# A hybrid GLA/HGRN2 layer on one core: the gate path ahead of the output projection, and the projection of two tiles by seven block products

## The chip, the cores and the metric

The kernel runs on one core of one Trainium2 chip. The metric is the device time of one execution in microseconds (us), lower is better. Each kernel was run several times; the profile is of one execution, taken by the hardware profiler. Five engines work beside each other, each on its own instructions in a fixed order: TensorE (PE; its weight loads are PEld), VectorE (DVE), ScalarE (ACT), GpSimd (POOL) and SyncE (SP), which only issues DMAs here.

## The reference

One inference step of a streaming encoder layer over 4096 prompt frames and 64 sample frames, width 1024, all in fp32. What matters for this change is its end:

```python
p = jnp.einsum('btd,de->bte', h, w_in)
q_a, k_a, v_a, z_a, a_lr, q_h, f_h, i_h, z_h = jnp.split(p, ...)
...                       # two gated recurrences give o_a and o_h, 512 wide each
o_a = rms_norm(o_a, g_on_gla).reshape(B, T, GLA_V) * jax.nn.silu(z_a)
o_h = rms_norm(o_h, g_on_hgrn).reshape(B, T, HGRN_W) * jax.nn.silu(z_h)
o = jnp.einsum('bte,ed->btd', jnp.concatenate([o_a, o_h], axis=-1), w_out)
y = x + gate[:, None] * rms_norm(o, g_post)
```

## The kernel before

Tokens are worked in 16 groups of 256, each two tiles of 128 tokens; the 64 sample frames ride as a third tile beside one group, so there are 33 tiles. Matrix products of fp32 data are made of three matmuls in a faster format, fp32r: each operand is split into a high part, rounded on ScalarE (`split`, L92), and a low part, the remainder, by a subtraction on VectorE or GpSimd (L93); high x high, high x low and low x high are summed in PSUM. With a gain the split is L89 on ScalarE and L90 on VectorE. For the half-full sample tile high and low part lie side by side in one operand, so that two matmuls do the work of three (`pair_step`), and `fold` adds the halves.

The program has three phases. The first runs the GLA heads over all groups, the second the HGRN2 heads; both write their outputs, normalised and (GLA) gated, to DRAM (`oa_d`, `oh_d`), and the normalised input is kept split-ready in DRAM as `h_d`. While a group's projections run, generators of other work are woven between them (`weave`: so many steps of a side, between so many steps of the main work). Phase 3 is the end: for each tile the projection z_h with its SiLU (`z_tile`: 24 matmuls of 512 columns from L620, sigmoid L1244, product L1245), the product with o_h (L1295), eight transposes (L1303), a split with the norm's gain (L89, L90), and the output projection, two halves of 512 columns with 24 matmuls each (L1338), square for the norm (L1343), scaling with gate (L1347), reciprocal root (`rstd`), product and residual (L1350) and store (L1352 or L1354).

The head of phase 3: four gate tiles are made while the last attention side of phase 2 and `load_wout` are woven in. `load_wout` loads w_out in 16 half rows of 128x512 (L1256) through a staging buffer `wst` and splits each, high part on ScalarE, low part on GpSimd, into eight units `wv` and eight `wu`. Then `phase3` alternates: one gate tile, then one tile's projection.

The framework's scheduler sets the order of each engine's instructions when the program is built; on the chip every engine runs its order, and waits where a semaphore is not there yet. All loads go through SyncE's queue in its order. Buffers come from pools of a fixed number of tiles: `hh` (split of a group's input, four used per group, five buffers), `hf` (its loads), PSUM banks `pj` (3), `at` (2), `tp`, `ms` and `o` (1 each), and the weight staging pool with two buffers of 128x1056, each of which serves two half rows.

In the profile's rows tiles are named without their number, so `wu` stands for all units of that name; L93 is the low part of a split, whatever is split. The lines are of this kernel; the new code's lines are those of the kernel after, where `split` is L93 and L94.

Of the kernel before, what the change touches and what calls it, by code (L numbers as in the profile page):

```python
# [28 lines left out]
class Kernel:  # L29
# [102 lines left out]
    def wunit(self, tag):  # L132
        return self.wpool.tile([P, 1056 if tag == "wv" else 1024], F32R, name=tag, bufs=8 if tag == "wv" else 16)


    def setup(self):
# [4 lines left out]
        self.wstage = self.pool(ctx, "wstage", 2)  # L141
        self.halves = []
        self.xp = self.pool(ctx, "x")
        self.hp = self.pool(ctx, "h")
        self.ep = self.pool(ctx, "e")
# [71 lines left out]
    def first_group(self, ap, ada, w, rows):  # L217
# [66 lines left out]
        def w_split(i, w):  # L284
            W[("qk", "z")[i]].append(self.split_w(w[i], ("wu", "wv")[i]))
# [62 lines left out]
        vs = self.weights(W["v"], C_VA, 512, "wu", self.etile, 3)  # L348
# [887 lines left out]
    def z_tile(self, h, r, o):  # L1236
        nc = self.nc
        pz = self.ps(self.z_bank)
        for _ in self.proj_tok(pz, self.W3["z"], 0, 512, h, o, r):
            yield  # L1240
# [8 lines left out]
    def load_wout(self, out):  # L1249

        sts = []
        for i in range(2 * KT + 2):
            if i < 2 * KT:
                kt, n = divmod(i, 2)
                st = self.wst()[:, :512]
                self.nc.sync.dma_start(st, self.t["w_out"][0, kt * P : (kt + 1) * P, 512 * n : 512 * n + 512])  # L1256
                sts.append(st)
            if i >= 2:
# [3 lines left out]
    def og_load(self, tile, og):  # L1262

        g, j, (kind, _, r, _) = tile
        g = g if kind == "p" else -1
        self.nc.sync.dma_start(og[:r, :512], self.oa_d[g][j])
        self.nc.sync.dma_start(og[:r, 512:], self.oh_d[g][j])

    def phase3(self, tiles, zgen, og):
        nc, t = self.nc, self.t  # L1270
        with ExitStack() as s:
            one = self.pool(s, "p3one")
            ap = self.pool(s, "p3a")
            gg = one.tile([P, 2, D], F32, name="gg")
            for i in range(2):
                nc.sync.dma_start(gg[:, i, :], self.gate_d[i : i + 1, :].to_broadcast([P, D]))
            Wo = self.W3["o"]
            og0 = og

            def load(i):  # L1280
                g, j, (kind, r0, r, o) = tiles[i]
                if i > 0:
                    og = ap.tile([P, D], F32, name="og", bufs=2)
                    self.og_load(tiles[i], og)
                else:
                    og = og0
                xt = self.xp.tile([P, D], F32, name="xt", bufs=2)
                src = t["x_prompt"] if kind == "p" else t["x_sample"]
                nc.sync.dma_start(xt[:r], src[0, r0 : r0 + r, :])
                return og, xt  # L1290

            def turn(i, og):
                r = tiles[i][2][2]
                e = self.zq.pop(0)
                nc.vector.tensor_tensor(og[:r, 512:], og[:r, 512:], e, ALU.mult)  # L1295
                hi = ap.tile([P, D], F32R, name="ogh", bufs=2).rearrange("p (k c) -> p k c", k=KT)
                lo = None
                if r == P:
                    lo = ap.tile([P, D], F32R, name="ogl", bufs=2).rearrange("p (k c) -> p k c", k=KT)
                for q, tag in enumerate(("tp", "ms")):  # L1300
                    pt = self.ps(tag).rearrange("p (k c) -> p k c", k=4)
                    for k in range(4):
                        nc.tensor.transpose(  # L1303
                            pt[:, k, :r], og[:r, (4 * q + k) * P : (4 * q + k + 1) * P], self.ident[:r, :r]
                        )
                    ks = slice(4 * q, 4 * q + 4)
                    self.split(hi[:, ks, :r], lo[:, ks, :r] if r == P else hi[:, ks, r : 2 * r], pt[:, :, :r], gain=self.col[:, 50 + q : 51 + q])
                return hi, lo

            n = len(tiles)  # L1310
            og, xt = load(0)
            next(zgen, None)
            hl = turn(0, og)
            for i in range(n):
                g, j, (kind, r0, r, o) = tiles[i]
                dst = t["y_prompt"] if kind == "p" else t["y_sample"]
                x_now, (hi, lo) = xt, hl
                if i + 1 < n:
                    next(zgen, None)
                    og, xt = load(i + 1)  # L1320
                    hl = turn(i + 1, og)
# [222 lines left out]
```

## Time and profile before

| what | value |
|---|---|
| time, median of 3 runs | 2156.81 us (2154.11 to 2157.73) |
| profiled execution | 2156.92 us |
| its span, first to last instruction | 2155.1 us |
| mean granted TensorE clock | 0.994 |
| bytes moved by DMA | 173.22 MB, mean 80 GB/s |
| last TensorE instruction of the output projection | starts at 2147.43 us of the span |
| last store issued | 2151.99 us |

The page's busy shares say how much of the span an engine works; the stretches (windows) say the same for parts of it, with the number of instructions in brackets. In a timeline row the columns are start, duration, engine, line, operation, output <- inputs, shape and count, and in square brackets the idle time ahead and what ended it. Matmul ends are modelled and overlap, so their pace is read from starts. A group's row ends with busy time in us and the mean of one in ns. A wait's row has total, count and longest in us.

### The profile page before, as it was taken

To read this page: it belongs to the slowest core of one execution; us is meant where nothing else is said; L and a number is where in the kernel's file an instruction comes from. 1 tells how busy PE (TensorE), PEld (TensorE's weight loads), DVE (VectorE), ACT (ScalarE), POOL (GpSimd) and SP (SyncE) were. 2 spreads that over 40 slices of the span, in tenths; PEclk is the share of its full clock that TensorE was granted. 3 is DMA by queue.
4 is the path that set the end of the run, shared out by engine and by line. 5 is a ranking of instruction groups with operands and counts; after the bars stand their busy time and mean duration, and the time that the engine had idled before them with its cause. 6 is when DMAs were issued, how large, how long until landed. Compare 5 with 4: busy or idle time off the path is not lost.

```text
span 2155.1 us, 44875 instructions
## 1 busy us (share of the span) xinstructions
PE 2109.0 (98%) x16574; PEld 1854.7 (86%) x16574; DVE 1502.3 (70%) x4851; ACT 993.3 (46%) x2960; POOL 234.2 (11%) x640
## 2 busy tenths in 40 slices
PE   8999999999999999999999999999999999999998
PEld 6888998889988888989999899999878888888887
DVE  6777777777777778787788887777895454545444
ACT  5666655666556654444444444444542222222212
POOL 3200010000100111110001110000240000000000
PEclk9999999999999999999999999999999999999999
DMA  9322222222222321012211101011253333334322
GB/s 262 112 58 74 63 58 50 66 66 62 57 50 62 111 93 47 31 31 70 65 51 45 36 31 50 31 36 43 91 161 130 120 123 108 127 115 131 110 100 88
DMA packets 218632, 173.22 MB, mean 80 GB/s; under 512 B 136236, under 2 KB 158224, under 8 KB 218412
## 3 DMA queue, kind: packets, MB, share of 16 engines
q1 hardware_dynamic: 218268, 170.08, 26.5%
q8 instruction: 131, 2.15, 0.4%
q14 instruction: 89, 0.73, 0.1%
q10 hardware_dynamic: 144, 0.26, 0.0%
HBM read 118.35 MB, written 51.93 MB: 79 GB/s over the span
## 4 chain that ended last, share of the span: by engine, by line
PE 82%; DVE 10%; ACT 4%; DMA 1%; issue 1%; SPq 1%; POOL 0%; DVEq 0%; ACTq 0%; POOLq 0%
PE ps_pj L620 22%; PE ps_pj L608 20%; PE ps_pj L1338 16%; PE ps_at L620 7%; PE ps_ms L840 2%; PE ps_o L824 2%; PE ps_o L819 2%; DVE wst L910 2%; PE ps_at L687 2%; PE ps_at L959 2%; PE ps_at L767 1%; PE ps_tp L794 1%; PE ps_tp L1303 1%; DVE dd L693 1%; PE ps_ms L1303 1%
## 5 line engine op out<-in xcount | busy, mean ns | idle before, releaser
L620 PE MATMUL ps_pj<-wu,hh 128*128 128x512 f32 x1632 | 405.2, 398 | 3.1 <-DVE hh L93 2.3
L608 PE MATMUL ps_pj<-hh,wu 128*128 128x256 f32 (+1 forms) x2976 | 392.1, 287 | 0.0
L608 PEld LDWEIGHTS ps_pj<-hh,wu 128*128 128x128 f32 x2976 | 372.8, 191 | 4.9 <-issue 0.3
L620 PEld LDWEIGHTS ps_pj<-wu,hh 128*128 128x128 f32 x1632 | 297.9, 188 | 65.8 <-issue 3.3
L608 PE MATMUL ps_pj<-hh,wv 128*128 128x256 f32 (+1 forms) x1536 | 214.7, 291 | 0.0
L608 PEld LDWEIGHTS ps_pj<-hh,wv 128*128 128x128 f32 x1536 | 193.2, 190 | 12.1 <-issue 9.3
L620 PE MATMUL ps_pj<-wv,hh 128*128 128x264 f32 x1464 | 199.3, 290 | 1.6 <-DVE wv L93 1.6
L620 PEld LDWEIGHTS ps_pj<-wv,hh 128*128 128x128 f32 x1464 | 184.1, 188 | 6.8 <-issue 2.4
L1343 ACT ACTIVATE sq<-ps_pj 128x512 bf16<-128x512 f32 (+1 forms) x66 | 39.4, 597 | 295.8 <-PE ps_pj L1338 294.3
L1338 PE MATMUL ps_pj<-wv,ogh 128*128 128x512 f32 x512 | 162.9, 399 | 0.0
L1338 PE MATMUL ps_pj<-wu,ogh 128*128 128x512 f32 x512 | 158.0, 390 | 0.0
L620 PE MATMUL ps_at<-wu,hh 128*128 128x512 f32 x672 | 157.7, 390 | 0.0
L1204 ACT ACTIVATE g<-ps_pj 128x256 f32<-128x256 f32 (+1 forms) x128 | 49.5, 387 | 229.5 <-PE ps_pj L608 228.8
L620 PEld LDWEIGHTS ps_at<-wu,hh 128*128 128x128 f32 x672 | 126.3, 188 | 26.1
L92 ACT CAST hh<-hf 128x512 fp32r<-128x512 f32 (+1 forms) x188 | 117.1, 626 | 68.5 <-PE ps_pj L620 38.7
L93 DVE TENSOR_TENSOR hh<-hf,hh 128x512 fp32r<-128x512 f32 (+1 forms) x188 | 130.7, 703 | 15.7 <-ACT hh L92 14.9
L941 POOL COPY T<-T 128x16 f32<-128x16 f32 (+1 forms) x32 | 9.9, 309 | 996.9 <-DVE Qg L880 893.2
L1338 PEld LDWEIGHTS ps_pj<-wu,ogh 128*128 128x128 f32 x512 | 96.1, 188 | 20.7
L1338 PEld LDWEIGHTS ps_pj<-wv,ogh 128*128 128x128 f32 x512 | 94.3, 189 | 19.3
L910 DVE TENSOR_TENSOR wst<-wst,T 128x160 f32<-128x160 f32 (+3 forms) x480 | 108.4, 267 | 1.1
L1338 PE MATMUL ps_pj<-wv,ogl 128*128 128x512 f32 x256 | 100.8, 394 | 0.0
L1338 PE MATMUL ps_pj<-wu,ogl 128*128 128x512 f32 x256 | 99.7, 390 | 0.0
(303 smaller groups left out, 3745.8 us busy)
## 6 DMA issues: line engine op xcount, KB each, us to landing
hf<-h_d SPq DMA_DIRECT2D x128, 256.0 KB
xt<-in_x_prompt_dram SPq DMA_DIRECT2D x36, 512.0 KB
h_d<-hf SPq DMA_DIRECT2D x64, 256.0 KB
out_y_prompt_dram<-y SPq DMA_DIRECT2D x31, 512.0 KB
xt<-in_x_prompt_dram SPq DMA_DIRECT2D x448, 32.0 KB
wst<-in_w_in_dram SPq DMA_DIRECT2D x36, 256.0 KB
ada_st<-in_w_ada_dram SPq DMA_DIRECT2D x32, 256.0 KB
oa_d<-e SPq DMA_DIRECT2D x32, 256.0 KB
```

Source lines behind the costliest of these rows:

```text
L92: self.nc.scalar.copy(hi, src)
L93: (eng or self.nc.vector).tensor_tensor(lo, src, hi.bitcast(F32), ALU.subtract)
L608: self.nc.tensor.matmul(ps[:, :T], a, b, start=i == 0, stop=i == n - 1)
L620: self.nc.tensor.matmul(ps[:r, : c1 - c0], a, b, start=kt == 0 and i == 0, stop=kt == KT - 1 and i == 2)
L687: nc.tensor.transpose(pt[:, i * P : (i + 1) * P], D[:, c + i, :], self.ident)
L819: nc.tensor.matmul(po[h], A[:, c * 4 + h, :], v, start=h < n, stop=St is None and h == 4 - n)
L824: nc.tensor.matmul(o, Q[rows[s], c * G + g, :], St[rows[s], g, :], start=NS == 2 and not apart and h == 1, stop=h == 4 - NS or h == 3 and ...
L840: nc.tensor.matmul(pd[s * w : (s + 1) * w, g, :], kc[:CL, g, s * w : (s + 1) * w], vs[c][:CL, h * P : (h + 1) * P], start=not apart, stop= ...
L910: nc.vector.tensor_tensor(parts(dst), parts(src), t.unsqueeze(3).to_broadcast(shape), ALU.mult)
L959: nc.tensor.matmul(pas[s][rows, g0 + g], K[rr, 2 * pr + g, rows], Yt[rr, o : o + P], start=True, stop=True)
L1204: nc.scalar.activation(sg, pf[:, :T], AF.Sigmoid)
L1338: nc.tensor.matmul(po[:r], a[:, kt, :r], b, start=m == 0, stop=m == 3 * KT - 1)
```

## The change

Phase 3 falls into two parts.

*Gate part.* All 33 gate tiles run one behind the other. Each loads its tile of o_h from DRAM, multiplies it by SiLU(z_h), and stores it back to the same place. Eight tiles are woven with the last attention side (spread over more steps than before); then 22 more are woven with `load_wout`. It now loads, for each of four block rows, two rows of 128x1024 (L1284), scales them by the norm's gain on ScalarE (L1285), takes four differences of their 512-wide halves on GpSimd (L1290) and splits seven operands (L93 on ScalarE, L94 on GpSimd): B11, B21, B22, T1, T2, T3, T4. That makes 28 units, 8 in `wv`, 8 in `wb` and 12 in `wc`. Of the differences each overwrites one of the staging buffers' halves.

*Projection.* Two tiles (256 tokens) are one 2x2 block matrix A (rows: the tiles; columns: GLA half and HGRN2 half), and w_out with its gain is a 2x2 block matrix B. Instead of eight block products, seven are made, each of 12 matmuls of 512 columns (L1336), of A's blocks and of sums of blocks: S1 = A21 + A22, S2 = S1 - A11, S3 = A11 - A21, S4 = A12 - S2. Sixteen transposes (L1327) bring the blocks to PSUM; VectorE makes the sums (L1357, L1363), and the results are put together from the products by additions from PSUM (L1408). The low parts of S1, S3 and S4 and two of the four scalings are on GpSimd, the rest on VectorE. Squares (L1396), scalings (L1399), the reciprocal root, now from ScalarE's table, product and residual (L1417) and stores of 512 columns (L1418) follow as before. The sample tile is projected inside the last pair with the prepared operands, in 40 matmuls instead of 32.

The buffers move as well: `wu` with 16 units becomes `wa` with 8 and `wb` with 8, some pools are allocated from the other side of the memory, and the pools of x and h are closed early to make room.

The diff, cut to its core:

```diff
-    def z_tile(self, h, r, o):
+    def z_tile(self, h, tile):
...
+        oh = self.etile()[:r]
+        nc.sync.dma_start(oh, o_d)
+        pz = self.ps("pj")
+        yield from self.proj_tok(pz, self.W3["z"], 0, 512, h, o, r)
...
         nc.vector.tensor_tensor(e, pz[:r], e, ALU.mult)
-        self.zq.append(e)
+        nc.vector.tensor_tensor(oh, oh, e, ALU.mult)
+        nc.sync.dma_start(o_d, oh)
...
-                st = self.wst()[:, :512]
-                self.nc.sync.dma_start(st, self.t["w_out"][0, kt * P : (kt + 1) * P, 512 * n : 512 * n + 512])
...
-                out.append(self.split_w(sts[i - 2], "wv" if i - 2 < 8 else "wu", self.nc.gpsimd))
...
+                st = self.stage_pair()[:, :D]
+                nc.sync.dma_start(st, self.t["w_out"][0, (4 * q + kt) * P : (4 * q + kt + 1) * P, :])
+                nc.scalar.activation(st, st, AF.Copy, scale=self.col[:, 50 + q : 51 + q])
...
+        for kt in range(4):
+            b11, b12, b21, b22 = load(kt)
...
+                self.split(us[n][:, 0], us[n][:, 1], src, nc.gpsimd)
...
+            put("B11", b11)
+            sub(b11, b12, b11)
+            sub(b12, b22, b12)
+            yield
+            put("B22", b22)
+            put("B21", b21)
+            sub(b22, b22, b11)
+            sub(b21, b21, b22)
+            yield
+            for n, src in (("T1", b11), ("T3", b12), ("T2", b22), ("T4", b21)):
+                put(n, src)
...
+        def product(bank, u, name):
+            for kt in range(4):
+                for i, (a, b) in enumerate(((0, 0), (0, 1), (1, 0))):
+                    nc.tensor.matmul(bank, u[:, a, kt, :], W[name][kt][:, b], start=kt + i == 0, stop=kt + i == 5)
...
+                product(b, cur["A11"], "B11")
...
+                product(b, cur["A12"], "B21")
+                y11 = add(self.etile(), b, p1)
+                square(ss[0], 0, y11)
+                scale(y11, y11, 0, eng=nc.gpsimd)
...
+                    parts(S3, w3, nc.gpsimd)
+                    parts(S1, w1, nc.gpsimd)
+                    parts(S2, w2)
...
+                product(b, cur["S2"], "T2")
+                u2 = add(tmp(), b, p1)
...
+                product(b, cur["S3"], "T3")
+                u3 = add(tmp(), b, u2)
...
+                    parts(S4, w4, nc.gpsimd)
...
+                product(b, cur["S1"], "T1")
+                y22 = add(self.etile(), b, u3)
...
+                scale(y22, y22, 1, eng=nc.gpsimd)
+                u4 = add(tmp(), b, u2)
...
+                product(b, cur["S4"], "B22")
+                y12 = add(self.etile(), b, u4)
...
+                product(b, cur["A22"], "T4")
+                y21 = add(self.etile(), b, u3)
...
-            self.weave(until(4), [(side, 15, 0, 12), (self.load_wout(W3["o"]), 18, 0, 12)])
...
+            self.weave(until(8), [(side, 15, 0, 22)])
...
+            self.weave(until(len(tiles) - 3), [(self.load_wout(room), 16, 0, 56)])
+            ogs = [self.og_half(0, j, q, self.ep if j else None) for j in range(2) for q in range(2)]
+            now(until(len(tiles) - 1))
+            self.project(ogs, lambda: now(zg))
```

More of the change, by code (lines that the diff above doesn't have):

```diff
@@ L1262, in og_load @@
[L1262 to L1270, printed above, removed]
-        with ExitStack() as s:
[L1272 to L1299, printed above, removed]
-                for q, tag in enumerate(("tp", "ms")):
[L1301 to L1305, printed above, removed]
-                    ks = slice(4 * q, 4 * q + 4)
[L1307 to L1321, printed above, removed]
-                cnd = 0 if kind == "p" else 1
-                ss = self.small.tile([P, 2], F32, name="y_ss")[:r]
-                y = ap.tile([P, D], F32, name="y", bufs=2)
-                if i == n - 1:
-                    self.tc.keep_in_program_order(nc.scalar.preload_act_table_set("natural_log_exp_and_others"))
@@ new lines, in load_wout, with unit, load, sub @@
+    def load_wout(self, room):
+        nc = self.nc
+        W = self.W3
+        names = ("B11", "B21", "B22", "T1", "T2", "T3", "T4")
+        for n in names:
+            W[n] = []
+        rooms = [("wv", i) for i in range(8)] + [("wb", i) for i in range(8)]
+        def unit():
+            u = self.wunit(rooms.pop(0)[0]) if rooms else room.tile([P, 1024], F32R, name="wc", bufs=12)
+            return u[:, :1024].rearrange("p (two c) -> p two c", two=2)
+        def load(kt):
+            sts = []
+            for q in range(2):
+                st = self.stage_pair()[:, :D]
+                nc.sync.dma_start(st, self.t["w_out"][0, (4 * q + kt) * P : (4 * q + kt + 1) * P, :])
+                nc.scalar.activation(st, st, AF.Copy, scale=self.col[:, 50 + q : 51 + q])
+                sts += [st[:, :512], st[:, 512:]]
+            return sts
+        def sub(dst, a, b):
+            nc.gpsimd.tensor_tensor(dst, a, b, ALU.subtract)
+        for kt in range(4):
+            b11, b12, b21, b22 = load(kt)
+            yield
+            us = {n: unit() for n in names}
+            def put(n, src):
+                self.split(us[n][:, 0], us[n][:, 1], src, nc.gpsimd)
[10 more added lines that the diff above has]
+                put(n, src)
+            for n in names:
+                W[n].append(us[n])
+            yield
@@ L1328, in phase3 @@
                 for q in range(2):
                     po = self.ps("pj")
-                    cs = slice(512 * q, 512 * q + 512)
-                    m = 0
-                    for kt in range(KT):
-                        wh, wl = Wo[2 * kt + q][:, 0], Wo[2 * kt + q][:, 1]
-                        if r < P:
-                            self.pair_step(po, hi[:, kt, : 2 * r], r, wh, wl, kt)
-                            continue
-                        for a, b in ((hi, wh), (hi, wl), (lo, wh)):
-                            nc.tensor.matmul(po[:r], a[:, kt, :r], b, start=m == 0, stop=m == 3 * KT - 1)
-                            m += 1
@@ new lines, in sample @@
+                    for i, (k, n) in enumerate(steps):
+                        b = both[:, k + 4 * (n[0] + n[1] == "B2"), : 2 * r]
+                        at = 0 if i == 0 else KT - 1 if i == len(steps) - 1 else 1
+                        self.pair_step(po, b, r, W[n][k][:, 0], W[n][k][:, 1], at)
+                    y = self.etile()[:r]
+                    self.fold(po, r, 512, y)
+                    square(ss, q, po[:r])
+                    nc.vector.tensor_tensor(y, po[:r], gs[q], ALU.mult)
@@ L1357, in weave, with og_half @@
+    def og_half(self, p, j, q, ap=None):
+        if ap is None:
+            o = self.ogp.tile([P, 512], F32, name="og", bufs=2)
+        elif ap is self.ep:
+            o = self.etile()
+        else:
+            o = ap.tile([P, 512], F32, name="ogb", bufs=2)
+        self.nc.sync.dma_start(o, (self.oa_d, self.oh_d)[q][p][j])
+        return o
     @staticmethod
```

238 lines of the change are left out of this document (181 added, 57 removed).

## Prediction

> **What bounds the kernel now.** The page comes first: TensorE is busy for 98% of the span.
>
> ```profile
> span 2155.1 us, 44875 instructions
> PE 2109.0 (98%) x16574; PEld 1854.7 (86%) x16574; DVE 1502.3 (70%) x4851; ACT 993.3 (46%) x2960; POOL 234.2 (11%) x640
> ```
>
> The profiled execution took 2156.92 us: 1.8 us lie outside its span, and it stands 0.1 us above the median of the three runs, 2156.81. I sum against it. Next, busy time by stretches: the last attention side with the weights of the projection, the start of phase 3, and its steady part.
>
> ```profile
> core 0: us, PE busy (x) PEld busy (x) DVE busy (x) ACT busy (x) POOL busy (x), PEclk, DMA share, GB/s
> 1560.00:1600.00 40.00, 38.02 (x280) 29.99 (x279) 36.36 (x99) 19.08 (x48) 17.45 (x24) 0.93 0.48 142
> 1600.00:1640.00 40.00, 37.26 (x169) 30.15 (x169) 26.28 (x68) 14.00 (x33) 5.30 (x11) 0.95 0.56 185
> 1700.00:1900.00 200.00, 200.00 (x928) 164.59 (x927) 97.99 (x262) 50.41 (x107) 0.00 (x0) 1.00 0.37 123
> 1900.00:2100.00 200.00, 200.00 (x929) 165.81 (x928) 97.35 (x270) 47.84 (x102) 0.00 (x0) 1.00 0.34 115
> ```
>
> From 1700 on TensorE never stops, VectorE is half used, GpSimd not at all: there each matmul taken away is worth its pace. Around 1560 to 1640 TensorE waits, and GpSimd works. The list of TensorE's waits from 1500 to 1660 (total, count, longest):
>
> ```profile
> PE ps_tp L1303 <- DMA og<-oa_d: 2.7, 1, 2.7
> PE ps_pj L620 <- DVE hh L93: 2.3, 1, 2.3
> PE ps_at L959 <- DVE wst L910: 1.6, 2, 1.3
> PE ps_o L824 <- DVE S L851: 1.1, 1, 1.1
> PE ps_o L819 <- ACT e L1155: 0.6, 1, 0.6
> ```
>
> **Matmuls: -45.** The timeline of TensorE gives the pace of a 512-wide matmul.
>
> ```profile
> 1634.77 0.61 PE L1338 MATMUL ps_pj<-wu,ogh 128*128 128x512 f32 x2
> 1637.49 0.62 PE L1338 MATMUL ps_pj<-wv,ogh 128*128 128x512 f32 x2
> 1640.28 0.63 PE L1338 MATMUL ps_pj<-wu,ogh 128*128 128x512 f32 x2
> ```
>
> Twelve on wu take 1637.49 - 1634.77 = 2.72 us (0.2267 each), twelve on wv 2.79 (0.2325). Two tiles cost 48 x 0.2325 + 48 x 0.2267 = 22.04 us now. Seven products of 12 make 84, 24 of them on wv; if wb and wc go like wu, that is 19.18 us, 2.86 less, and 45.8 over 16 pairs. If they go like wv it is 84 x 0.2325 = 19.53, and 40.2. I take 45. Gate matmuls and transposes keep their number. The sample takes 40 paired matmuls for 32: 8 x 0.23 = **+1.8**.
>
> **Waits that go: -5.** The 2.7 us wait for og at the head of phase 3 vanishes, since 33 gate tiles now stand there. It has an after-effect, which the wait for hh shows best:
>
> ```profile
> 1559.61 1.88 PE L620 MATMUL ps_pj<-wu,hh 128*128 128x512 f32 x4 [2.26 <-DVE hh L93]
> 1561.29 1.91 PE L687 MATMUL ps_at<-ident,A 128*128 128x128 f32 x8
> 1562.85 3.18 PE L620 MATMUL ps_pj<-wu,hh 128*128 128x512 f32 x12
> 1631.11 0.60 PE L1303 MATMUL ps_tp<-ident,og 128*128 128x128 f32 x4
> 1631.55 0.60 PE L1303 MATMUL ps_ms<-ident,og 128*128 128x128 f32 x4
> ```
>
> Four matmuls take 1.68 us, 0.42 each, so after 2.26 us of idleness TensorE restarts at about half pace; (0.42 - 0.227) x 4 = 0.8 on them, and about as much on the transposes behind (8 in 1.56, 0.2 each, against 4 in 1631.55 - 1631.11 = 0.44): about 1.4 a stall. So 2.7 + 1.4 go, and some of the smaller waits, because the last attention side spreads over eight tiles instead of four: bounds 0 and -8, taken -5. By the Trainium skill ("TensorE: Matmul & The Clock Gate", "What's actually happening") the clock halves only after an idle window of about 3.4 us; the 2.26 us row disagrees, and the measurement decides, though the same page calls the window free-running.
>
> **Weight preparation: +27, the term that decides.** Now GpSimd splits eight half rows per weight half: 16 lo parts. After, each of four block rows needs 7 lo parts and 4 differences on GpSimd, one behind the other. GpSimd's order before, in the middle of the splitting (wst a staging buffer with half a row, wv and wu the operands):
>
> ```order
> L93 TENSOR_TENSOR wv_22055<-wst_22014,wv_22055 128x512
> L93 TENSOR_TENSOR wv_22123<-wst_22014,wv_22123 128x512
> L93 TENSOR_TENSOR wu_22128<-wst_22053,wu_22128 128x512
> L93 TENSOR_TENSOR wu_22164<-wst_22053,wu_22164 128x512
> L93 TENSOR_TENSOR wu_22271<-wst_22126,wu_22271 128x512
> L93 TENSOR_TENSOR wu_22275<-wst_22126,wu_22275 128x512
> ```
>
> A staging buffer is left behind two operations. This is GpSimd's order after, the third block row (wst_22924 and wst_22927 are its two staging buffers; wb and wc the operands):
>
> ```order
> L94 TENSOR_TENSOR wb_22962<-wst_22924,wb_22962 128x512
> L1290 TENSOR_TENSOR wst_22924<-wst_22924 128x512
> L1290 TENSOR_TENSOR wst_22924<-wst_22927,wst_22924 128x512
> L94 TENSOR_TENSOR wc_22964<-wst_22927,wc_22964 128x512
> L94 TENSOR_TENSOR wb_22963<-wst_22927,wb_22963 128x512
> L1290 TENSOR_TENSOR wst_22927<-wst_22927,wst_22924 128x512
> L94 TENSOR_TENSOR wc_22965<-wst_22924,wc_22965 128x512
> L1290 TENSOR_TENSOR wst_22927<-wst_22927 128x512
> L94 TENSOR_TENSOR wc_22967<-wst_22924,wc_22967 128x512
> L94 TENSOR_TENSOR wc_22966<-wst_22927,wc_22966 128x512
> L94 TENSOR_TENSOR wc_22968<-wst_22927,wc_22968 128x512
> ```
>
> The staging buffer wst_22924 is free for the next row only behind the ninth. On ScalarE, at the same place, the gate part and the weights share one order (e is a gate tile's sigmoid, hh the split of its input). Before, a steady stretch of phase 3:
>
> ```order
> L1244 ACTIVATE e_22701<-ps_at_22676 128x512
> L89 ACTIVATE ogh_22710<-ps_tp_22712,col_168 128x512
> L89 ACTIVATE ogh_22710<-ps_ms_22719,col_168 128x512
> L1343 ACTIVATE sq_22753,y_ss_22726<-ps_pj_22728 128x512
> L1343 ACTIVATE sq_22781,y_ss_22726<-ps_pj_22756 128x512
> L92 CAST hh_22933<-hf_22669 128x512
> ```
>
> After, at the second and third block row:
>
> ```order
> L93 CAST wb_22736<-wst_22673 128x512
> L93 CAST wb_22735<-wst_22676 128x512
> L93 CAST wb_22737<-wst_22676 128x512
> L1252 ACTIVATE e_22628<-ps_pj_22603 128x512
> L93 CAST hh_22682<-hf_22594 128x512
> L1285 ACTIVATE wst_22924<-wst_22924,col_168 128x1024
> L93 CAST hh_22685<-hf_22595 128x512
> L1285 ACTIVATE wst_22927<-wst_22927,col_168 128x1024
> L93 CAST hh_22688<-hf_22596 128x512
> L93 CAST wb_22962<-wst_22924 128x512
> ```
>
> So hh_22685, which the next gate tiles' matmuls need, stands behind the scaling of wst_22924 (L1285), which waits for a DMA, which waits for GpSimd to leave that buffer. If GpSimd is late, ScalarE stands, then TensorE. SyncE's queue, which issues that DMA, waits as well, and behind it stand the next loads of h and the store of a gate tile; the store's own wait for VectorE's product (0.69 us behind the sigmoid's) costs nothing while the h loads run a group, 10.9 us, ahead. GpSimd's pace, its groups by form and its timeline:
>
> ```profile
> L93 POOL TENSOR_TENSOR wu<-wst,wu 128x512 fp32r<-128x512 f32 x9 | 13.9, 1552 | 0.6 <-ACT wu L92 0.6
> L93 POOL TENSOR_TENSOR wv<-wst,wv 128x512 fp32r<-128x512 f32 x8 | 13.1, 1661 | 20.2 <-ACT wv L92 20.2
> 1590.61 7.25 POOL L93 TENSOR_TENSOR wu<-wst,wu 128x512 fp32r<-128x512 f32 x4
> 1598.26 2.57 POOL L93 TENSOR_TENSOR wu<-wst,wu 128x512 fp32r<-128x512 f32 x2 [0.40 <-ACT wu L92]
> ```
>
> A mean of 1.61 us, 1.28 alone, 1.81 in company. No row shows a subtraction there; I price it as a lo part, the same two inputs. Eleven make 17.7 us a block row. The reload, from SyncE's issue to ScalarE's cast, and a 1024-wide ScalarE pass:
>
> ```profile
> 1594.39 1.40 SPq L1256 DMA_DIRECT2D wst<-in_w_out_dram  x2
> 1597.57 0.62 ACT L92 CAST wu<-wst 128x512 fp32r<-128x512 f32 x1 [1.20 <-DMA wst<-in_w_out_dram]
> L92 ACT CAST ada_h<-ada_st 128x1024 fp32r<-128x1024 f32 x16 | 16.6, 1039 | 0.7 <-DMA ada_st<-in_w_ada_dram 0.7
> ```
>
> 3.2 us for 256 KB, some 3.6 for 512 KB, + 1.04 + 0.62 = 5.3; less the two GpSimd operations still running, 3.2, leaves 2.1. A row takes 19.8 us. ScalarE's order puts three sigmoids between the first scalings of the second and third rows, two between the third and fourth, and about one and a half up to the fourth's last cast. A gate tile is 24 x 0.227 = 5.45 us, so TensorE has 16.4, 10.9 and 8.2 us of work against 19.8, 19.8 and nine operations (14.5): waits of 3.4, 8.9 and 6.3, and 1 or 2 in the first row, 20 us. Five stalls restart at 1.4: +7. Together **27**. At 1.28 the row is 14.1 + 2.7 = 16.8, the waits 0.4, 5.9, 3.3, and D about 16 with restarts. At 1.81 it is 19.9 + 1.7 = 21.6: 5.2, 10.7, 8.1, 2 and restarts, 33. Were the restarts free, as the skill's window of 3.4 us would have it for the shorter stalls, it is 20.
>
> **The rest: +2.7.** From gate to pairs, the first pair's loads arrive about when needed: 0 to 3, taken 1. The gate part moves 0.52 MB of hf and twice 0.26 MB of oh a tile, 1.05 MB in 5.45 us = 191 GB/s. The page's first slice shows 262 GB/s:
>
> ```profile
> DMA  9322222222222321012211101011253333334322
> GB/s 262 112 58 74 63 58 50 66 66 62 57 50 62 111 93 47 31 31 70 65 51 45 36 31 50 31 36 43 91 161 130 120 123 108 127 115 131 110 100 88
> ```
>
> so its DMAs stay hidden, at nothing; uncovered, 33 tiles at 262 GB/s last 132 us, under their 180 us of matmuls. In a pair VectorE has 21 operations and 10 tiny ones:
>
> ```profile
> L1350 DVE SCALAR_TENSOR_TENSOR y<-y,nwt_y,xt 128x512 f32<-128x512 f32 x62 | 43.9, 749 | 1.1
> L1347 DVE TENSOR_TENSOR y<-ps_pj,gg 128x512 f32<-128x512 f32 x61 | 41.9, 687 | 41.6 <-ACT sq L1343 41.6
> L83 DVE SCALAR_TENSOR_TENSOR nwt_y<-nwt_u,nwt_y 128x1 f32<-128x1 f32 x91 | 14.5, 160 | 3.1
> 1590.59 0.81 DVE L93 TENSOR_TENSOR hh<-hf,hh 128x640 fp32r<-128x640 f32 x1
> 1594.83 1.89 DVE L93 TENSOR_TENSOR hh<-hf,hh 128x640 fp32r<-128x640 f32 x1
> 1596.65 1.11 DVE L851 SCALAR_TENSOR_TENSOR S<-S,T,ps_ms 128x128 f32<-128x128 f32 x4
> ```
>
> 21 x 0.7 + 10 x 0.16 = 16.3 us, under TensorE's 84 x 0.228 + 16 x 0.11 = 20.9. While GpSimd ran (1590.61 on), the lo part of hh, with two inputs from SBUF, took 1.89 for 0.81, while L851, which reads PSUM, kept 0.28. Seven of the 21 have two SBUF inputs (four L1417, two L1399, the lo of S2); GpSimd has five operations, 8 us a pair. At odds of 8/20.9 and 0.8 us each that delays VectorE by 2 us a pair, inside its slack: 0 to 5 over all pairs, taken 1. The end has one more addition ahead of the last square: +0.7 as in L1347.
>
> **Sum.** -45 + 1.8 - 5 + 27 + 1 + 1 + 0.7 = -18.5, from 2156.9: **2138.4 us**. With the low ends 2156.9 - 45.8 + 1.8 - 8 + 16 + 0.7 = 2121.6; with the high ends 2156.9 - 40.2 + 1.8 + 33 + 3 + 5 + 0.7 = 2160.2. All high ends at once are unlikely: the forecast's own range is 2122 to 2151.
>
> **Rivals.**
> - *The preparation is hidden.* If the gate part's ring of five hh buffers and its PSUM banks let TensorE run ahead while ScalarE stands, 2 us of stall stay: 2138.4 - 25 = 2113. For it: GpSimd needs 79 us, the gate part lasts 180. Against: the order quoted, with gate splits between the weights. Chance 0.14.
> - *Stalls without half pace*, as the skill's clock page would make most of these: 2138.4 - 7 = 2131. Against: 1559.61. Chance 0.06.
> - *GpSimd subtracts at twice the price of a lo part.* 4 x 1.61 more a row, 6.4, on three rows: +19, 2157.6: nothing won. For: no row shows one. Against: same inputs. Decides from 3 us an operation. Chance 0.08.
> - *VectorE becomes the bound in the pairs, slower.* If every GpSimd operation keeps VectorE out, 16.3 + 8 = 24.3 against 20.9: 3.4 x 16 = +54, 2193. It decides once VectorE is held over 4.6 us a pair. For: 1594.83. Against: L851; fourteen of its operations read PSUM. The Trainium skill ("SBUF — State Buffer", "SBUF: two separate sides") says that a VectorE operation with two SBUF inputs and a GpSimd operation that reads SBUF lock each other out for a whole instruction, and it speaks against this change, which puts GpSimd into a part where it was idle; the rows agree. Chance 0.08.
>
> The forecast keeps 0.64.
>
> **Numbers.** A measurement here can tell about 0.2%, 4.3 us: the same is 2152.5 to 2161.1. Faster: 0.64 + 0.14 + 0.06, and a little of the third rival, 0.85. Same: 0.06, most of that rival. Slower: the fourth and a trace of the third, 0.09. The range 2113 to 2155 leaves out the fourth, half of the third and the first's lower side, some 0.18.
>
> **What would show it.** Right: pairs of about 21 us with TensorE full; three to five TensorE waits in the gate part, put down to hh or ScalarE, beside L1285 waiting for DMA and GpSimd's 44 operations without a gap. Wrong: no waits there (2113), L1290 rows near 3 us, or TensorE waiting in every pair for VectorE.

## The result, and the profile after

The kernel after takes 2135.48 us (median of 4 runs, 2132.65 to 2136.53) against 2157.01 us before (4 runs, 2154.11 to 2157.73): a ratio of 0.9901, 95% interval 0.9883 to 0.9918, some 21 us. The profiled execution of the kernel after took 2135.26 us, its span 2133.4; that of the kernel before had a span of 2155.1, so the two traces differ by 21.7 us. The forecast was 2138.4.

The page of the kernel after shows TensorE busy for 35 us less (2109.0 before) and GpSimd for 142 us more (234.2 before):

```profile
span 2133.4 us, 45130 instructions
PE 2073.7 (97%) x16390; PEld 1817.6 (85%) x16390; DVE 1563.9 (73%) x4742; ACT 1061.4 (50%) x3124; POOL 376.2 (18%) x745
```

By stretches: the weight preparation inside the gate part (1620 to 1700), the undisturbed gate part, and the pairs. The last two rows are short pieces of the first two.

```profile
core 0: us, PE busy (x) PEld busy (x) DVE busy (x) ACT busy (x) POOL busy (x), PEclk, DMA share, GB/s
1620.00:1660.00 40.00, 34.18 (x123) 24.89 (x122) 23.30 (x21) 19.77 (x33) 27.73 (x19) 0.87 0.60 197
1660.00:1700.00 40.00, 29.76 (x113) 22.92 (x112) 18.87 (x21) 16.49 (x29) 25.07 (x19) 0.87 0.49 153
1700.00:1740.00 40.00, 40.00 (x178) 33.14 (x177) 19.76 (x30) 12.49 (x22) 0.00 (x0) 1.00 0.61 196
1900.00:2100.00 200.00, 200.00 (x946) 164.88 (x946) 144.21 (x298) 77.65 (x198) 62.79 (x46) 1.00 0.44 145
1651.00:1657.50 6.50, 5.59 (x13) 3.92 (x13) 3.17 (x4) 4.21 (x7) 2.85 (x2) 0.50 0.78 268
1668.00:1674.60 6.60, 4.39 (x10) 3.34 (x11) 4.19 (x4) 3.39 (x5) 3.73 (x3) 0.50 0.90 285
```

Where 40 us hold 178 matmuls undisturbed, they hold 123 and 113 while GpSimd prepares the weights: 120 fewer in all, or 27 us at 40/178 us each. The granted clock of 0.87 is a mean of full and half: by stretches of 1 us it is 0.50 in four pieces (the two shown are the longer ones, of 6.8 us each; the others, from 1623.4 and from 1688.3, last 3.4 us each), 20.5 us in all. The pairs are full, VectorE at 72% in them. TensorE's waits from 1500 on are now three rows, two of them in the gate part (total, count, longest):

```profile
PE ps_pj L624 <- ACT hh L93: 8.7, 5, 3.0
PE ps_pj L624 <- DVE hh L94: 7.3, 5, 2.3
PE ps_at L963 <- DVE wst L914: 1.3, 1, 1.3
```

The wait for og and those for S, e and A of the kernel before are gone; ten waits for hh, 16.0 us, have come. ScalarE's timeline shows what stands ahead of the splits of hh:

```profile
1625.47 1.15 ACT L1285 ACTIVATE wst<-wst,col 128x1024 f32<-128x1024 f32 x1 [3.22 <-POOL wv L94]
1633.31 1.15 ACT L1285 ACTIVATE wst<-wst,col 128x1024 f32<-128x1024 f32 x1 [4.47 <-DMA wst<-in_w_out_dram]
1634.37 0.60 ACT L93 CAST hh<-hf 128x512 fp32r<-128x512 f32 x1
...
1648.60 1.15 ACT L1285 ACTIVATE wst<-wst,col 128x1024 f32<-128x1024 f32 x1 [4.25 <-POOL wb L94]
1649.66 0.60 ACT L93 CAST hh<-hf 128x512 fp32r<-128x512 f32 x1
...
1663.04 0.62 ACT L93 CAST wc<-wst 128x512 fp32r<-128x512 f32 x1 [3.14 <-POOL wst L1290]
1665.50 0.62 ACT L93 CAST wc<-wst 128x512 fp32r<-128x512 f32 x1 [1.84 <-POOL wst L1290]
1666.52 0.61 ACT L93 CAST hh<-hf 128x512 fp32r<-128x512 f32 x1
```

The scalings (L1285) of the last three block rows wait 1 to 4.5 us each, for GpSimd or for the reload, and mostly a split of hh follows at once. The longest waits of TensorE stand at another place of the same order: the casts of the differences (into wc) wait for GpSimd's subtractions (L1290), and the split of hh at 1666.52, with a sigmoid between, comes behind them. Four waits, 10.2 of the 16.0 us, follow these casts in the third and the fourth row. GpSimd's timeline has the rows' beginnings:

```profile
1627.35 1.30 POOL L94 TENSOR_TENSOR wv<-wst,wv 128x512 fp32r<-128x512 f32 x1 [1.92 <-ACT wv L93]
1654.57 1.29 POOL L94 TENSOR_TENSOR wb<-wst,wb 128x512 fp32r<-128x512 f32 x1 [5.98 <-ACT wb L93]
1672.39 1.28 POOL L94 TENSOR_TENSOR wc<-wst,wc 128x512 fp32r<-128x512 f32 x1 [2.79 <-ACT wc L93]
```

The second, third and fourth block rows begin at 1627.35, 1654.57 and 1672.39: 27.2 and 17.8 us apart, where 19.8 was reckoned. TensorE's timeline has the first matmuls of a run of 600 (25 gate tiles) that holds all ten waits, a restart, two of the longest waits, and the transposes behind the run:

```profile
1606.52 13.77 PE L624 MATMUL ps_pj<-wa,hh 128*128 128x512 f32 x60
1650.31 2.80 PE L624 MATMUL ps_pj<-wa,hh 128*128 128x512 f32 x6 [1.61 <-ACT hh L93]
1667.18 0.73 PE L624 MATMUL ps_pj<-wa,hh 128*128 128x512 f32 x2 [3.04 <-ACT hh L93]
1670.20 12.78 PE L624 MATMUL ps_pj<-wa,hh 128*128 128x512 f32 x46 [2.30 <-DVE hh L94]
1769.96 0.60 PE L1327 MATMUL ps_tp<-ident,e 128*128 128x128 f32 x4
```

After 1.61 us of waiting six matmuls take up 2.80 us, against 1.52 us for six at full pace (the last row of the next view). The run of 600 takes 1769.96 - 1606.52 = 163.4 us.

A pair's period is read from the transposes that open it (L1327), and TensorE's last group:

```profile
1801.06 0.60 PE L1327 MATMUL ps_tp<-ident,ogb 128*128 128x128 f32 x4
1822.14 0.60 PE L1327 MATMUL ps_tp<-ident,ogb 128*128 128x128 f32 x4
...
2121.45 1.52 PE L1336 MATMUL ps_pj<-wc,wa 128*128 128x512 f32 x6
```

One pair takes 21.08 us. In the kernel before, two tiles without their gate tiles take 2 x 11.86, from the last transposes there:

```profile
2101.12 0.60 PE L1303 MATMUL ps_tp<-ident,og 128*128 128x128 f32 x4
2112.98 0.60 PE L1303 MATMUL ps_tp<-ident,og 128*128 128x128 f32 x4
```

So a pair saves 23.72 - 21.08 = 2.64 us, 42.2 in all.

### The profile page after: what moved, and what is told of

It is laid out like the page before. It is cut to its first block, busy times and chain, and to the rows that moved or that the text cites. A ratio compares the mean times of both kernels' runs of the same rounds, so it can differ in the third digit from the quotient of the medians.

```text
span 2133.4 us, 45130 instructions
## 1 busy us (share of the span) xinstructions
PE 2073.7 (97%) x16390; PEld 1817.6 (85%) x16390; DVE 1563.9 (73%) x4742; ACT 1061.4 (50%) x3124; POOL 376.2 (18%) x745
## 4 chain that ended last, share of the span: by engine, by line
PE 80%; DVE 9%; ACT 4%; POOL 2%; DMA 2%; issue 2%; SPq 1%; DVEq 0%; ACTq 0%; POOLq 0%
PE ps_pj L624 28%; PE ps_pj L612 21%; PE ps_pj L1336 12%; PE ps_ms L844 2%; PE ps_o L828 2%; PE ps_o L823 2%; PE ps_o L1336 2%; PE ps_at L691 2%; PE ps_at L963 2%; DVE wst L914 2%; PE ps_at L771 1%; PE ps_tp L798 1%; POOL wst L1290 1%; DMA wst<-in_w_in_dram 1%; ACT A L781 1%
## 5 line engine op out<-in xcount | busy, mean ns | idle before, releaser
L612 PE MATMUL ps_pj<-hh,wa 128*128 128x256 f32 (+1 forms) x2976 | 392.1, 287 | 0.0
L624 PE MATMUL ps_pj<-wb,hh 128*128 128x512 f32 x1536 | 378.8, 396 | 0.9 <-ACT K L1043 0.9
L612 PEld LDWEIGHTS ps_pj<-hh,wa 128*128 128x128 f32 x2976 | 372.7, 191 | 4.9 <-issue 0.3
L624 PEld LDWEIGHTS ps_pj<-wb,hh 128*128 128x128 f32 x1536 | 280.3, 188 | 59.1 <-issue 2.7
L612 PE MATMUL ps_pj<-hh,wv 128*128 128x256 f32 (+1 forms) x1536 | 213.2, 289 | 0.0
L624 PE MATMUL ps_pj<-wa,hh 128*128 128x512 f32 x768 | 190.1, 406 | 16.1 <-ACT hh L93 8.7
L612 PEld LDWEIGHTS ps_pj<-hh,wv 128*128 128x128 f32 x1536 | 191.8, 188 | 12.1 <-issue 9.3
L624 PEld LDWEIGHTS ps_pj<-wa,hh 128*128 128x128 f32 x768 | 147.2, 195 | 53.9 <-ACT hh L93 11.8
L94 DVE TENSOR_TENSOR hh<-hf,hh 128x512 fp32r<-128x512 f32 (+1 forms) x188 | 140.5, 756 | 41.9 <-ACT hh L93 40.9
L93 ACT CAST hh<-hf 128x512 fp32r<-128x512 f32 (+1 forms) x188 | 116.9, 624 | 68.6 <-PE ps_pj L624 52.8
L914 DVE TENSOR_TENSOR wst<-wst,T 128x160 f32<-128x160 f32 (+4 forms) x480 | 108.5, 266 | 1.1
L1396 ACT ACTIVATE sq<-e 128x512 bf16<-128x512 f32 x64 | 40.4, 631 | 119.1 <-DVE e L1408 116.1
L1336 PE MATMUL ps_pj<-wc,wa 128*128 128x512 f32 x384 | 98.3, 391 | 0.0
L1399 POOL TENSOR_TENSOR e<-e,gg 128x512 f32<-128x512 f32 x32 | 41.4, 1293 | 294.5 <-ACT sq L1396 178.5
L938 ACT ACTIVATE A<-Ac,member 128x128 f32<-128x128 f32 x256 | 80.8, 390 | 24.4 <-DVE Ac L932 24.4
L947 POOL TENSOR_TENSOR T<-T,T 128x16 f32<-128x16 f32 (+1 forms) x224 | 83.8, 374 | 17.0
L1336 PEld LDWEIGHTS ps_pj<-wc,wa 128*128 128x128 f32 x384 | 72.0, 188 | 16.0
```

Of the source, the lines that this page charges most:

```text
L93: self.nc.scalar.copy(hi, src)
L94: (eng or self.nc.vector).tensor_tensor(lo, src, hi.bitcast(F32), ALU.subtract)
L612: self.nc.tensor.matmul(ps[:, :T], a, b, start=i == 0, stop=i == n - 1)
L624: self.nc.tensor.matmul(ps[:r, : c1 - c0], a, b, start=kt == 0 and i == 0, stop=kt == KT - 1 and i == 2)
L914: nc.vector.tensor_tensor(parts(dst), parts(src), t.unsqueeze(3).to_broadcast(shape), ALU.mult)
L938: nc.scalar.activation(Ah[:, :, 32 * b : 32 * b + 32], Ach, AF.Copy, scale=self.member[:CL, 8 + b : 9 + b])
```

## The experiments

The theory: the seven products save about 43 us; GpSimd's long chain for each block row, with ScalarE's scaling and its splits in one order, gives back 27 of them in the gate part. Rivals: the gate part's own traffic causes the waits, or GpSimd's work and VectorE's cost time in the pairs. Every kernel is compared with the kernel before on its own chip, so kernels are set against each other by these ratios (0.001 is 2.2 us).

**The differences on VectorE.**

```diff
         def sub(dst, a, b):
-            nc.gpsimd.tensor_tensor(dst, a, b, ALU.subtract)
+            nc.vector.tensor_tensor(dst, a, b, ALU.subtract)
```

> The kernel after with the four differences of each block row of w_out on VectorE instead of GpSimd; nothing else. Theory of the prediction (GpSimd's eleven operations a block row hold the staging buffers, and ScalarE's scaling and with it the gate part wait for them): GpSimd has 7 operations a row, 7 x 1.5 = 10.5 us, the row with its reload about 14 us instead of 18 to 20, against 10.9 to 16.4 us of gate matmuls between two scalings: the ten TensorE waits of the gate part shrink from 16 us to some 5, and the time falls by 12 to 18 us, to 2117 to 2123. Rival (the waits come from the traffic of the gate part: loads of h, loads and stores of o_h, loads of w_out): no change, 2133 to 2138.

Measured: 2122.24 us, ratio 0.9853 (0.9836 to 0.9869) against 0.9901, some 10 us less. In the profiled execution the gate part ends 15.3 us earlier, but its run of 600 matmuls begins 5.2 us earlier already (1601.37), and takes 153.3 us for 163.4: 10.1 us less. The waits are 12.3 us, mostly now for VectorE's low part of hh:

```profile
PE ps_pj L624 <- DVE hh L94: 9.8, 5, 2.9
PE ps_pj L624 <- ACT hh L93: 2.5, 2, 2.0
```

GpSimd's length counts, as the theory has it, but the move brings VectorE into the same chain: the gain lies below what was expected.

**The preparation held in program order on ScalarE.** Scalings and high parts of w_out are pinned behind what precedes them in the program; the weaving, unchanged, spreads them.

```diff
-                nc.scalar.activation(st, st, AF.Copy, scale=self.col[:, 50 + q : 51 + q])
+                self.tc.keep_in_program_order(nc.scalar.activation(st, st, AF.Copy, scale=self.col[:, 50 + q : 51 + q]))
...
-                self.split(us[n][:, 0], us[n][:, 1], src, nc.gpsimd)
+                hi, lo = us[n][:, 0], us[n][:, 1]
+                self.tc.keep_in_program_order(nc.scalar.copy(hi, src))
+                nc.gpsimd.tensor_tensor(lo, src, hi.bitcast(F32), ALU.subtract)
```

> The kernel after with ScalarE's scalings and high parts of w_out held in program order, so that about six gate tiles instead of two or three stand between the scalings of two block rows on ScalarE; the same operations on the same engines, the same bytes. Theory: six tiles are 33 us against a row of 18 to 20, so ScalarE no longer waits for GpSimd with the gate part's splits behind it: the waits and their restarts at half pace go, some 24 us, 2110 to 2115. Rival one (GpSimd's work or the traffic as such costs TensorE, wherever it stands): no change, 2133 to 2138. Rival two (restarts cost nothing, only the waits do): 16 us, 2119.

Measured: 2109.85 us, ratio 0.9791 (0.9776 to 0.9806). The same operations and bytes, 24 us less. The same waits and stretches as above, of this kernel:

```profile
PE ps_pj L624 <- ACT hh L93: 1.6, 1, 1.6
PE ps_pj L624 <- DVE hh L94: 1.1, 1, 1.1
```

```profile
1620.00:1660.00 40.00, 38.77 (x168) 31.13 (x168) 26.24 (x25) 20.81 (x36) 26.81 (x18) 1.00 0.59 194
1660.00:1700.00 40.00, 38.39 (x166) 30.48 (x164) 27.38 (x28) 19.11 (x32) 21.93 (x14) 1.00 0.70 232
```

GpSimd is nearly as busy, the bytes per second are as many in the first stretch and more in the second, the granted clock is 1.00, and TensorE does 168 and 166 matmuls instead of 123 and 113. The run of 600 takes 140.8 us. So it is the order on ScalarE, and neither the work nor the traffic by itself, that makes the stall. Both rivals fall: 13.3 us of waits went, and 24 us of time.

**Without o_h in the gate part.**

```diff
-        nc.sync.dma_start(oh, o_d)
...
-        nc.vector.tensor_tensor(oh, oh, e, ALU.mult)
-        nc.sync.dma_start(o_d, oh)
```

> The kernel after without the load, the product and the store of o_h in the gate part (so o_h stays without its gate): 17 MB less traffic, 33 VectorE products and 66 DMAs less. Theory (transfers are hidden, the weight preparation sets the waits): 2130 to 2137. Rival (the gate part's traffic, 191 GB/s and w_out, causes the waits): 10 us or more less, 2125 or below.

Measured: 2120.99 us, ratio 0.9843 (0.9828 to 0.9857), 12 us less. Here the expectation failed: what I had put down at nothing cost 10 us (the run of 600 takes 153.2 us for 163.4) to 12 us (by the ratios) of the 27. GpSimd's block rows are 19 us apart in this kernel:

```profile
1622.70 1.29 POOL L94 TENSOR_TENSOR wv<-wst,wv 128x512 fp32r<-128x512 f32 x1 [2.16 <-ACT wv L93]
1641.84 1.26 POOL L94 TENSOR_TENSOR wb<-wst,wb 128x512 fp32r<-128x512 f32 x1 [2.52 <-ACT wb L93]
1660.69 1.28 POOL L94 TENSOR_TENSOR wc<-wst,wc 128x512 fp32r<-128x512 f32 x1 [2.79 <-ACT wc L93]
```

The row that took 27.2 us in the kernel after is the one with the difference. SyncE's timeline of the kernel after shows what stands ahead of its reload:

```profile
1622.07 0.33 SPq L1284 DMA_DIRECT2D wst<-in_w_out_dram  x1
1622.50 2.13 SPq L580 DMA_DIRECT2D hf<-h_d  x3
1624.68 0.42 SPq L1246 DMA_DIRECT2D e<-oh_d  x1
1626.01 0.32 SPq L580 DMA_DIRECT2D hf<-h_d  x1
1626.61 0.32 SPq L1255 DMA_DIRECT2D oh_d<-e  x1
1627.03 0.38 SPq L1284 DMA_DIRECT2D wst<-in_w_out_dram  x1
```

The second staging buffer's load stands behind four loads of h, a load of o_h and a store of it, is issued at 1627.03, and its data reach ScalarE at 1633.31: 6.3 us, where the first took at most 3.4.

**The same, taken apart.** First the transfers alone (the tile of o_h is stored as loaded), then the product alone (the gate with itself, and no DMA):

```diff
-        nc.vector.tensor_tensor(oh, oh, e, ALU.mult)
         nc.sync.dma_start(o_d, oh)
```

> The kernel after without the product of o_h with its gate in the gate part: the tile of o_h is loaded and stored again unchanged, so all transfers stay and 33 VectorE operations go. Leaving out transfers and product together had saved about 13 us. If the transfers, or their places in SyncE's queue, cost that: no change against the kernel after, 2131 to 2137. If the product on VectorE costs it (two inputs from SBUF, locked out by GpSimd, with the low parts of hh behind it, or the store that waits for it in SyncE's queue): 2119 to 2124.

```diff
-        nc.sync.dma_start(oh, o_d)
...
-        nc.vector.tensor_tensor(oh, oh, e, ALU.mult)
-        nc.sync.dma_start(o_d, oh)
+        nc.vector.tensor_tensor(e, e, e, ALU.mult)
```

> The kernel after without the loads and stores of o_h in the gate part, but with a product of the same size on VectorE, of the gate with itself (o_h stays without its gate). If the transfers or their places in SyncE's queue cost the 13 us: 2119 to 2124. If VectorE's product costs them: 2131 to 2137. About half way in both this run and the one without the product: both count.

Measured: 2129.34 us, ratio 0.9871 (0.9856 to 0.9885), and 2128.61 us, 0.9864 (0.985 to 0.9879): each about 7 us less than the kernel after, half way. The run of 600 takes 159.8 and 159.9 us, 3.6 less each, where both edits together give 10.3. So both count, and by the traces part of the gain comes only when both are gone. In the trace without the product the waits for VectorE's low parts of hh fall from 7.3 to 2.0 us while those for ScalarE's grow from 8.7 to 10.7; how much of the product's share is the store that waits for it in SyncE's queue stays open.

**Without o_h, with the preparation pinned.** The two edits above together.

> The pinned kernel without the load, the product and the store of o_h in the gate part (o_h stays without its gate). In the kernel after, leaving these out saved about 12 us. Theory (they cost only by lengthening the reload of the staging buffers, and the low parts of hh, while the weight preparation holds ScalarE): with the preparation spread out nothing is left to save, ratio to the kernel before 0.976 to 0.980, against 0.979 of the pinned kernel. Rival (they take time from the gate part of themselves, by traffic or VectorE): 12 us less again, 0.973 to 0.974.

Measured: 2104.6 us, ratio 0.9762 (0.9746 to 0.9779), 6 us below the pinned kernel: inside the theory's range at its low end, and half of what the rival asks. No wait for hh is left in its trace, and its run of 600 takes 136.0 us, 4.8 less than the pinned kernel's. That is the pinned kernel's last 2.7 us of waits, and 2.1 us whose cause stays open: the granted clock is 1.00 in both. So transfers and product cost where the splits of hh come late, and the traces show no cost elsewhere.

**Twelve more matmuls in each pair.**

```diff
                 product(b, cur["A22"], "T4")
+                product(b, cur["A22"], "T4")
```

> The kernel after with the last of the seven products of a pair done twice into the same bank (the result overwrites itself): 12 more matmuls in each of 16 pairs, what an eighth product would cost. Theory: 12 x 0.23 x 16 = 44 us, 2177 to 2181, since TensorE sets the pairs' time. Rival (VectorE, ScalarE or loads set the pairs' time, TensorE has room): less than 30 us.

Measured: 2176.45 us, ratio 1.0101 (1.0086 to 1.0116), 43 us more: TensorE sets the pairs' time, and an eighth product costs its whole matmuls.

**GpSimd out of the pairs.**

```diff
-                scale(y11, y11, 0, eng=nc.gpsimd)
+                scale(y11, y11, 0)
...
-                    parts(S3, w3, nc.gpsimd)
-                    parts(S1, w1, nc.gpsimd)
+                    parts(S3, w3)
+                    parts(S1, w1)
...
-                    parts(S4, w4, nc.gpsimd)
+                    parts(S4, w4)
...
-                scale(y22, y22, 1, eng=nc.gpsimd)
+                scale(y22, y22, 1)
```

> The kernel after with GpSimd's five operations of each pair (two scalings, the low parts of S1, S3 and S4) on VectorE. VectorE works 144 us of 200 in the pairs, 15.2 us of a pair's 21.1; five more make 18.7, still under it. Theory (TensorE sets the pairs): within 3 us of the kernel after, the change at the end of the last pair. Rival (the lock between VectorE and GpSimd costs time in the pairs): 5 us or more faster. Other rival (VectorE's order is too tight, 18.7 of 21.1 makes TensorE wait in each pair): 16 us or more slower.

Measured: 2133.66 us, ratio 0.9888 (0.9874 to 0.9903), 3 us less, inside the interval of the kernel after. The pair's period is the same 21.08 us (1797.63 to 1818.71 in its trace), with VectorE busy for 153 us of 180. The gate part, in which nothing was edited, ends 3.4 us earlier in this profiled execution, but not by its stalls: the run of 600 takes 163.3 us, as in the kernel after, and begins earlier. The difference is there in the first 86 us of the program, where the first matmul of L612 starts at 81.6 us, and at 85.6 in the kernel after. Neither rival holds: the lock costs no time that shows in the pairs, and moving work to GpSimd saves nothing there.

**The last attention side in four gate tiles, as before.**

```diff
-            self.weave(until(8), [(side, 15, 0, 22)])
+            self.weave(until(4), [(side, 15, 0, 12)])
+            now(until(8))
```

> The kernel after with the last attention side woven into four gate tiles, as before, instead of eight; nothing else. Theory (that TensorE's waits at the end of the recurrence went because this side was spread): the waits of the kernel before for hh, wst, S and e, about 4 us more than are left, come back with restarts: 3 to 7 us more, 2137 to 2143. Rival (they went because the split of w_out no longer stands there): no change, 2133 to 2137.

Measured: 2139.14 us, ratio 0.9917 (0.99 to 0.9933), 3.5 us more by the ratios, while the intervals overlap. Its trace has more waits for hh (19.8 us against 16.0), and the waits for S, e and A of the kernel before did not come back. Its run of 600 takes 170.6 us, 7.2 more. So in the trace the spreading is worth something, though not for the reason I gave, and most of what went at the end of the recurrence did not go by it.

**Eight plain products in two parts**, pinned: the gate part of the change alone.

```diff
-        names = ("B11", "B21", "B22", "T1", "T2", "T3", "T4")
+        names = ("B11", "B12", "B21", "B22")
...
+                def block_of(j, q):
+                    b = self.ps("pj")
+                    product(b, cur[f"A{j + 1}1"], f"B1{q + 1}", last=False)
+                    product(b, cur[f"A{j + 1}2"], f"B2{q + 1}", first=False)
+                    y = self.etile()
+                    square(ss[j], q, b)
+                    scale(y, b, q)
+                    ys[j, q] = y
```

> The pinned kernel with eight plain block products (96 matmuls a pair, of the parts of A11, A12, A21, A22 and of B11, B12, B21, B22, added in PSUM), without the sums of blocks, the differences of w_out and their splits, and with 32 matmuls for the sample: the gate part of the change alone. Theory: 12 x 0.229 x 16 = 44 us more than the pinned kernel, less some 2 of the sample, 1 or 2 of waits in the gate part and 2 of the tail: 0.979 x 2157 + 38 = 2150, 0.995 to 0.999 of the kernel before. Rival (the seven products cost elsewhere what they save, in VectorE or loads): under 2135, 0.990 or less.

Measured: 2144.82 us, ratio 0.9944 (0.9931 to 0.9958), 33 us above the pinned kernel and 12 below the kernel before: just under the range expected, and far from the rival's. In its trace a pair takes 23.74 us, and the run of 600, without a wait, 136.0 us from here to the transposes at 1742.70:

```profile
1606.69 136.17 PE L624 MATMUL ps_pj<-wa,hh 128*128 128x512 f32 x600
```

```profile
1779.11 0.60 PE L1324 MATMUL ps_tp<-ident,ogb 128*128 128x128 f32 x4
1802.85 0.60 PE L1324 MATMUL ps_tp<-ident,ogb 128*128 128x128 f32 x4
```

Its pairs cost what two tiles cost in the kernel before (23.72), and its end after the last matmul as well (7.6 us), so its span of 2143.5 gives the removed waits by itself: 2143.5 - 2155.1 = -11.6 us. It also gives the rest: 34.2 us lie between it and the pinned kernel's span of 2109.3, and 16 x 2.65 = 42.4 of matmuls less 1.9 of the sample (40 matmuls in 9.25 us, 32 in 7.38), 3.2 of the end and 3.2 by which the pinned kernel's first product starts later make 34.1. The 3.2 are 4.8 of stall left, less a run of 600 that begins 1.6 us earlier.

**The sample one product earlier in the last pair**, pinned.

```diff
+                if not more:
+                    ogs, *rest_s = load_sample()
                 b = self.ps("pj")
                 product(b, cur["A11"], "B11")
...
+                else:
+                    both = turn_sample(ogs)
 
                 b = self.ps("pj")
                 product(b, cur["S2"], "T2")
...
+                else:
+                    sample(both, *rest_s)
 
                 b = self.ps("pj")
                 product(b, cur["S3"], "T3")
```

> The kernel with the pinned weight preparation, and in the last pair the sample tile is loaded before the pair, transposed ahead of the third product and projected ahead of the fourth, one product earlier. In the kernel after 10 us follow the last matmul, 7.5 in the kernel before, and VectorE takes up the last product about 1.5 us late, with the sample's last operations just ahead of it. Theory (the longer tail is VectorE's backlog from the sample): 1.5 to 3 us off the pinned kernel's ratio of 0.979, 0.9775 to 0.9785. Rival (the tail is the chain of the last product itself: addition, square, root, product, store): no change, 0.979.

Measured: 2111.2 us, ratio 0.979 (0.9776 to 0.9804): no change that can be measured. In the traces the stretch from the last matmul's start (five paces into its last group) to the end of the span falls from 10.8 to 9.4 us, VectorE takes the last product up at once, and then puts two other operations (L1419) ahead of the last scaling, which gives some of it back. Its pairs begin 1.4 us later.

## Why the prediction was right, point by point

The traces' difference of 21.7 us divides as follows, beside the terms of the forecast.

| term | forecast | measured | from |
|---|---|---|---|
| matmuls of the pairs | -45 | -42.2 | pair periods, 16 x 2.64 |
| sample | +1.8 | +1.9 | 9.25 us, against 7.38 for 32 matmuls in eight plain products |
| waits that go | -5 | -11.6 | eight plain products in two parts |
| weight preparation | +27 | +27.2 | the remainder; the run of 600 takes 163.4 us, 136.0 undisturbed: 27.4 |
| gate to pairs | +1 | 0 | no wait in the list |
| lock in the pairs | +1 | 0 | no wait in the list; same period without GpSimd |
| the end | +0.7 | +3.1 | 10.8 against 7.7 us from the start of the last matmul |

*Matmuls.* The mechanism held, and the size was near: 84 matmuls go at 0.230 us, between the two paces seen before. The eighth product's price, 43 us, says the same from the other side.

*Waits that go.* Mis-sized by more than its bounds. The kernel before waits 8.3 us from 1500 to 1660 in the five kinds shown, and 0.5 in a sixth, for A; I let the og wait go with its restart and only some of the rest. Of all of them 1.3 us are left, so 7.5 went, and with their restarts 11.6. The reason I gave, the wider spreading, is not borne out: with the side in four tiles the old waits stayed away. The other difference there is that the split of w_out no longer stands beside the recurrence; that was not tried by itself.

*Weight preparation.* The size is right as a whole, and its parts err on both sides. Waits: 16.0 us where 20 were reckoned; restarts: 27.2 - 16.0 = 11.2 where 7 were. They are not a fixed price of each wait: the clock is halved in four pieces beside ten waits, and 20.5 us at half clock explain at most 10.2 of the 11.2. The forecast's sign, three to five waits and GpSimd without a gap, did not come so: there were ten waits, and GpSimd stood for 1.9 to 6.0 us at each new row and for 4.1 in the second. The waits were put behind the scalings, which wait for the reload; most of the time went behind the casts of the differences, which wait for GpSimd itself. GpSimd was a little quicker, a subtraction as dear as a low part, as these groups of the kernel after show:

```profile
L1290 POOL TENSOR_TENSOR wst<-wst 128x512 f32<-128x512 f32 x16 | 23.3, 1459 | 17.7 <-ACT wst L1285 17.1
L94 POOL TENSOR_TENSOR wc<-wst,wc 128x512 fp32r<-128x512 f32 x12 | 16.9, 1429 | 2.8 <-ACT wc L93 2.8
```

That settles the rival of the double price: 1.46 against 1.43 us. A row of eleven is 16 us and not 17.7; the reload was longer than the 3.6 us reckoned, 6.3 in the second row. Here a step failed: "so its DMAs stay hidden, at nothing". They are hidden by bandwidth (197 and 153 GB/s beside the 262 of the first slice before), and not for the one load that a staging buffer waits for, which stands behind them in the same queue. Some 10 to 12 of the 27 us would not be there without o_h's transfers and product. The main claim, that GpSimd's chain reaches TensorE through the order on ScalarE, is shown by the pinned kernel: same work, 24 us less.

*Hidden preparation, as a rival* (2113): it fell for this kernel, and it is what the pinned kernel makes true, at 2110.

*Stalls without half pace, as a rival* (2131): it fell, by the granted clock of 0.50 in the rows shown.

*VectorE as the bound.* It fell: 72% in the pairs, and 85% without GpSimd, with the same period. The lock itself is seen, where it costs 0.9 us: in the last pair an operation of one column takes 1.07 us and ends with GpSimd's scaling (1.28 us from 2119.17), and 0.14 us in the kernel without GpSimd there. VectorE's timeline of the kernel after, then of the other:

```profile
2119.40 1.07 DVE L82 SCALAR_TENSOR_TENSOR nwt_u<-nwt_y 64x1 f32<-64x1 f32 x1 [0.53 <-ACT nwt_y L77]
```

```profile
2116.26 0.14 DVE L82 SCALAR_TENSOR_TENSOR nwt_u<-nwt_y 64x1 f32<-64x1 f32 x1
```

*The end.* Mis-sized: not one addition but a queue. VectorE takes the last product up late, behind the sample's last operations and the scaling of the block before, and both tiles' results still pass it:

```profile
2120.87 1.41 DVE L1417 SCALAR_TENSOR_TENSOR work<-e,nwt_y,work 64x512 f32<-64x512 f32 x2
2122.20 0.68 DVE L1408 TENSOR_TENSOR e<-ps_pj,tmp 128x512 f32<-128x512 f32 x1
2123.67 0.69 DVE L1399 TENSOR_TENSOR e<-e,gg 128x512 f32<-128x512 f32 x1 [0.79 <-ACT sq L1396]
2124.35 0.68 DVE L1408 TENSOR_TENSOR e<-ps_pj,tmp 128x512 f32<-128x512 f32 x1
```

So the forecast came within 3 us partly because errors cancelled: 6.6 us more went at the head and 2 of small costs did not come, against 2.8 us less from the matmuls and 2.4 more at the end.

*The clock rule.* By the Trainium skill ("TensorE: Matmul & The Clock Gate", "What's actually happening") an idle window of about 3.4 us halves the clock. The length agrees with these traces, where the clock is 0.50 for 3.4 or 6.8 us at a time. That it takes an idle window does not: none of the ten waits was longer than 3.04 us, and the piece from 1650.7 follows a wait of 1.61. The measurement decides.

## What to carry to other kernels

Seven products for eight pay their full eighth as long as TensorE sets the pace, and what must be prepared for them is part of the price: here 27 of 42 us, made of waits for an engine that is 18% busy and of what such waits do to the clock. Where an engine serves two streams in one fixed order, ask which of them can be late, and put enough of the other stream between its instructions: the pinned kernel gets back 24 us by order alone, and at 0.979 of the kernel before it is, with its variant of the last pair, the fastest here that leaves nothing out. A transfer that bandwidth hides still delays the load behind it in its queue, if somebody waits for that load.

## What the runs showed of the hardware that was not expected

Waits of 1 to 3 us in rapid order can halve TensorE's clock, in pieces of 3.4 us or twice that: beside ten waits of 16.0 us the granted clock was 0.50 for 20.5 us, and the run of 600 matmuls took 27.4 us longer. Not every wait does it: the pinned kernel kept a clock of 1.00 beside waits of 1.1 and 1.6 us.

The price of a stall repeats well: the run of 600 took 163.4, 164.0 and 163.3 us in the kernel after, with twelve more matmuls and without GpSimd in the pairs, which share their gate part. What differs between profiled executions lies elsewhere, and most of it early: the first matmul of L612 starts between 81.3 and 86.1 us in the kernel after and its eleven variants. So stretches of two traces are better compared from a common mark than by the times at which they end.
